# A first load of 8 rows for 16, and ScalarE's padding drains one row group sooner, in a low-rank-adapted linear layer

## The chip, the cores, the metric

One core of a Trainium2 chip. The metric is the device time of one execution in microseconds (us), the median of several runs. The profiled execution's span is some 1.3 us shorter than its time. All times inside a span count from the span's start.

## The reference

```python
# x: 16 x 2048 x 256 float32; W: 256 x 256; lora_A: 256 x 16; lora_B: 16 x 256; lora_E: 16; scale = 1.0
x_flat = x.reshape(-1, in_dim)
y = x_flat @ W
lora_out = ((x_flat @ lora_A) * lora_E) @ lora_B
y = y + scale * lora_out
```

The kernel folds the low-rank part into one 256 x 256 weight, `weff`, and then multiplies x by it. It reads 33.6 MB of x and writes 33.6 MB of y.

## The kernel before

32,768 rows are cut into 4 chunks, each of 64 rows on each of 128 partitions (8.4 MB). Three "homes" in on-chip memory hold a chunk each; y overwrites x in its home. A chunk is computed in 16 groups of 4 rows: GpSimd casts a group to bf16, TensorE transposes it, VectorE copies the result out of PSUM (the memory that TensorE writes), TensorE multiplies, ScalarE copies y back to the home. SyncE issues nearly all loads and stores, in the order of a list, on one queue, called the ring below; 16 transfer engines serve it.

```python
ORDER = [
    ("A",),
    ("L", 0, 0, 16), ("L", 0, 16, 40), ("L", 0, 40, 64),   # load chunk 0: rows 0 to 16, ...
    ("L", 1, 0, 32), ("L", 1, 32, 64),
    ("L", 2, 0, 64),
    ("S", 0, 0, 40), ("S", 0, 40, 64),                     # store chunk 0
    ("L", 3, 0, 32), ("L", 3, 32, 64),                     # into chunk 0's home
    ("S", 1, 0, 64), ("S", 2, 2, 62), ("S", 3, 0, 64),
]
HELD = (2, 0)                    # GpSimd holds chunk 2 back ...
HOLDERS = (("S", 0, 0, 40),)     # ... until this store has landed
VECTOR_DRAINS, GPSIMD_DRAINS, SCALAR_DRAINS = 12, 10, 22
# ... (cut)
    def drain(engine, n):
        for op, landed in loaded.items():
            if op[1:3] == HELD:
                engine.wait_ge(landed, 16)
        for _ in range(n):
            engine.drain()

    def scalar_program():
        # ... (cut: set-up loads of W, B, E)
        for g in range(N_GROUPS):
            c, b = g // GPC, g % GPC * CG
            if (c, b) == HELD:
                drain(scalar, SCALAR_DRAINS)
            scalar.wait_ge(s_y, g + 1)
            scalar.copy(out=home(c)[:, b:b + CG, :], in_=psum_y[g % NY][:]).then_inc(s_free[(g + NY) % UNROLL], 1)
            # ... (cut)
            if g in ends:
                scalar.drain().then_inc(s_done, 1)      # lets SyncE issue a store

    # TensorE, for each group i (cut): turn(i + 1, i), then multiply(i).
    # turn(i + 1) waits for GpSimd's cast of group i + 1; its last transpose waits for the y buffer of group i.
```

The wait of GpSimd at HELD is called the hold. The drains do no work. They pad each engine's stream of instructions, so that the place where one page of instructions ends and the next begins (a crossing) falls into the hold.

The edge rows of chunk 2 (0, 1, 62, 63) go out on GpSimd's own queue in three unequal shares.

## Time and profile before

| | before |
|---|---|
| time, median of 6 runs | 161.25 us (161.09 to 161.41) |
| span of the profiled run | 160.0 us |
| transfers, all queues, share of 16 engines' span | 98.9% |
| first landing of x / chunk 2 landed / first store landed | 8.09 / 62.70 / 75.04 us |
| ScalarE's drains | 80.23 to 81.42 us |
| last store issued / landed | 122.82 / 159.99 us |

Some numbers below come from the trace's packet records (start, duration, size and queue of each). "Excess" below is the time by which packets of 1024 bytes or more take longer than 9 ns + 0.03676 ns a byte (the line through the medians of 611 ns for 16,384 bytes and 2418 ns for 65,536), summed and divided by 16 engines.

### The profile page before, as it was taken

How to read it: one execution, taken by the hardware profiler on the slowest of the kernel's cores; microseconds unless marked ns; L12 is line 12 of the kernel's file. 1: busy time of each engine (PE TensorE's matmuls, PEld its weight loads, DVE VectorE, ACT ScalarE, POOL GpSimd, SP SyncE). 2: the span in 40 equal slices, each digit the busy share in tenths (PEclk: the TensorE clock that was granted, in tenths of full speed). 3: DMA queues.
4: the chain of work that ended last, by engine and by line, in shares of the span. 5: the costliest groups of instructions: out<-in, count | busy, mean ns of one | idle time of the engine just before them, and what ended most of it. 6: DMA issues, size and time to landing. Idle time of an engine off the chain costs nothing.

```text
span 160.0 us, 2070 instructions
## 1 busy us (share of the span) xinstructions
PE 96.5 (60%) x782; PEld 84.4 (53%) x782; DVE 45.4 (28%) x66; ACT 66.0 (41%) x65; POOL 69.3 (43%) x73
## 2 busy tenths in 40 slices
PE   2769999999999900000999999999994000000000
PEld 1246899999999900000789999999993000000000
DVE  0113355555555500000155555555550000000000
ACT  3001477777777720000257777777775000000000
POOL 1072577777787400002577777778762000000000
PEclk9999999999999995555599999999999555555555
DMA  7999999999969997999999999989979997989986
GB/s 269 427 448 436 412 440 467 451 393 418 631 262 524 475 311 328 403 420 434 412 465 428 401 475 426 532 377 410 524 308 446 480 485 305 544 342 481 441 360 262
DMA packets 2451, 67.43 MB, mean 421 GB/s; under 512 B 512, under 2 KB 528, under 8 KB 784
## 3 DMA queue, kind: packets, MB, share of 16 engines
q1 hardware_dynamic: 2016, 66.60, 97.4%
q0 software_dynamic: 224, 0.52, 0.9%
q10 hardware_dynamic: 208, 0.28, 0.6%
q14 instruction: 3, 0.02, 0.0%
HBM read 33.85 MB, written 33.55 MB: 421 GB/s over the span
## 4 chain that ended last, share of the span: by engine, by line
PE 38%; DMA 33%; ACT 3%; POOL 1%; issue 1%; ACTq 0%; SPq 0%
DMA out_dram<-home 28%; PE psum_y L269 24%; PE psum_xt L258 13%; DMA home<-in_x_dram 5%; ACT home L221 3%; POOL stage L200 1%; PE psum_y L291 1%; SPq L147 0%; ACTq L175 0%; ACTq L225 0%
## 5 line engine op out<-in xcount | busy, mean ns | idle before, releaser
L200 POOL CAST stage<-home 128x1024 bf16<-128x1024 f32 x64 | 66.6, 1042 | 48.6 <-PE psum_xt L258 22.1
L221 ACT COPY home<-psum_y 128x1024 f32<-128x1024 f32 x64 | 64.7, 1012 | 54.8 <-PE psum_y L269 54.8
L269 PE MATMUL psum_y<-weff,xt 128*128 128x256 bf16 x512 | 69.1, 280 | 0.0
L242 DVE COPY xt<-psum_xt 128x1024 bf16<-128x1024 bf16 x64 | 44.3, 692 | 66.2 <-PE psum_xt L258 66.2
L258 PE MATMUL psum_xt<-ident,stage 128*128 128x128 f32 x260 | 42.2, 286 | 22.3 <-POOL stage L200 22.3
L269 PEld LDWEIGHTS psum_y<-weff,xt 128*128 128x128 bf16 x512 | 51.5, 101 | 6.2
L258 PEld LDWEIGHTS psum_xt<-ident,stage 128*128 128x128 f32 x260 | 32.4, 148 | 25.2 <-issue 23.6
L282 PE MATMUL psum_y<-ident 128*128 128x512 f32 x4 | 3.8, 1101 | 2.9 <-POOL ident L180 2.9
L282 PEld LDWEIGHTS psum_y<-ident 128*128 128x128 f32 x4 | 1.2, 325 | 3.9 <-POOL ident L180 2.9
L230 DVE TENSOR_SCALAR ate<-psum_y,e_sb 16x256 f32<-16x256 f32 x1 | 0.5, 471 | 7.2 <-DMA e_sb<-in_lora_E_dram 7.2
L168 POOL DMA_DIRECT2D out_dram<-home x3 | 2.0, 676 | 1.0 <-PE psum_xt L258 1.0
L221 ACT ACT_TABLE_LOAD x1 | 1.3, 1283 | 2.1 <-SPq L304 2.1
L291 PE MATMUL psum_y<-b_sb,ate 16*128 16x256 f32 x4 | 2.1, 670 | 0.0
L291 PEld LDWEIGHTS psum_y<-b_sb,ate 16*128 16x128 f32 x4 | 1.2, 320 | 0.5 <-issue 0.3
L246 DVE TENSOR_TENSOR weff<-w_sb,psum_y 128x512 bf16<-128x512 f32 x1 | 0.7, 689 | 1.4 <-PE psum_y L291 1.4
L285 PEld LDWEIGHTS psum_y<-ident,a_sb 128*16 128x16 f32 x2 | 0.3, 138 | 1.2 <-issue 1.2
L178 POOL MEMSET ident<- 128x128 f32 x1 | 0.2, 205 | 1.7 <-SPq L304 1.7
L285 PE MATMUL psum_y<-ident,a_sb 128*16 128x128 f32 x2 | 0.6, 421 | 0.0
L180 POOL TENSOR_SCALAR_AFFINE_SELECT ident<-ident 128x128 f32<-128x128 f32 x1 | 0.3, 284 | 0.2 <-POOL ident L178 0.2
L326 POOL MEMSET const-float32-0.0<- 128x1 f32 x1 | 0.1, 94 | 0.2 <-issue 0.2
L326 POOL MEMSET const-bfloat16-1.0<- 128x1 bf16 x1 | 0.1, 97 | 0.0
L326 POOL MEMSET const-uint8-127<- 128x1 uint8 x1 | 0.1, 97 | 0.0
(1 smaller groups left out, 0.1 us busy)
## 6 DMA issues: line engine op xcount, KB each, us to landing
home<-in_x_dram SPq DMA_DIRECT2D x4, 4096.0 KB, 24.4
out_dram<-home SPq DMA_DIRECT2D x1, 7680.0 KB, 38.0
home<-in_x_dram SPq DMA_DIRECT2D x2, 3072.0 KB, 16.8
out_dram<-home SPq DMA_DIRECT2D x1, 5120.0 KB, 45.2
out_dram<-home SPq DMA_DIRECT2D x1, 3072.0 KB, 44.6
home<-in_x_dram SPq DMA_DIRECT2D x1, 2048.0 KB, 7.7
out_dram<-home POOLq DMA_DIRECT2D x1, 432.0 KB, 30.2
w_sb<-in_W_dram ACTq DMA_DIRECT2D x1, 256.0 KB, 2.8
```

Source lines behind the costliest of these rows:

```text
L168: engine.dma_start(out=ends_of(y_chunks[SHARED]), in_=ends_of(home(SHARED))).then_inc(landed, 16)
L200: gpsimd.tensor_copy(out=stage[g % NS][:], in_=home(c)[:, b:b + CG, :]).then_inc(s_stage[g % UNROLL], 1)
L221: scalar.copy(out=home(c)[:, b:b + CG, :], in_=psum_y[g % NY][:]).then_inc(s_free[(g + NY) % UNROLL], 1)
L230: vector.tensor_scalar(out=ate[:], in0=psum_y[0][:R, :KT, :P], scalar1=e_sb[:], scalar2=float(scale), op0=ALU.mult, op1=ALU.mult,).then_in ...
L242: vector.tensor_copy(out=xt[g % NX][:], in_=psum_xt[g % NT][:].bitcast(BF16)).then_inc(s_xt[g % UNROLL], 1)
L246: vector.tensor_add(out=weff[:], in0=w_sb[:], in1=psum_y[1][:, :KT, :]).then_inc(s_free[0], 1)
L258: ins = tensor.transpose(psum_xt[i % NT][:, b, :], words[:, b, :], ident[:])
L269: ins = tensor.matmul(psum_y[i % NY][:, b, :], xt[i % NX][:, b, t::KT], weff[:, t, :], start=(t == 0), stop=(t == KT - 1),)
L282: tensor.matmul(psum_y[1][:, :2, :], ident[:], ident[:, None, :].to_broadcast([P, 4, P]), start=True, stop=True)
L285: ins = tensor.transpose(psum_y[0][:R, t, :P], a_sb[:, t, :], ident[:])
L291: ins = tensor.matmul(psum_y[1][:, t, :], ate[:, t, :], b_sb[:], start=True, stop=True)
L326: nc = _bacc.Bacc("TRN2", target_bir_lowering=False, num_devices=1)
```

## The change

It is meant to start compute sooner, by a smaller first load, and to take ScalarE's drains off the path that leads out of the hold: they stand before the copy of group 31, which waits for the hold, instead of behind it.

```diff
-    ("L", 0, 0, 16),
-    ("L", 0, 16, 40),
-    ("L", 0, 40, 64),
+    ("L", 0, 0, 8),
+    ("L", 0, 8, 32),
+    ("L", 0, 32, 64),
@@
-SCALAR_DRAINS = 22
+SCALAR_DRAINS = 26
@@
-            if (c, b) == HELD:
+            if (c, b + CG) in (HELD, (HELD[0] - 1, HELD[1] + ROWS)):
                 drain(scalar, SCALAR_DRAINS)
```

## The prediction

> **What bounds the kernel now.** I first read the page's slices and its queue lines: is any engine, or the transfer engines, full for the whole span?
>
> ```profile
> PE   2769999999999900000999999999994000000000
> POOL 1072577777787400002577777778762000000000
> DMA  7999999999969997999999999989979997989986
> ...
> q1 hardware_dynamic: 2016, 66.60, 97.4%
> q0 software_dynamic: 224, 0.52, 0.9%
> q10 hardware_dynamic: 208, 0.28, 0.6%
> q14 instruction: 3, 0.02, 0.0%
> ```
>
> The compute engines have two empty stretches: a hold at about 57 to 75 us, and everything after 123 us. The DMA row has none, and its queues sum to 98.9% of 16 engines' span. The transfers are the bound: x in and y out, 67.1 MB that no part of this change alters. Is the rate full in every stage? Windows give, at the end of each line, granted clock, DMA share and GB/s (a packet counts where it begins, hence shares just over 1):
>
> ```profile
> 0.00:2.00 2.00, 0.00 (x0) 0.00 (x0) 0.00 (x0) 0.00 (x0) 0.20 (x4) 1.00 0.43 111
> 2.00:40.00 38.00, 34.86 (x239) 28.07 (x240) 14.60 (x22) 19.21 (x19) 22.57 (x24) 1.00 1.01 432
> 40.00:80.00 40.00, 19.99 (x167) 18.05 (x166) 9.43 (x15) 14.33 (x15) 14.28 (x15) 0.74 1.00 420
> 80.00:120.00 40.00, 39.95 (x366) 36.95 (x365) 21.15 (x31) 30.25 (x31) 31.18 (x31) 1.00 1.01 435
> 120.00:158.00 38.00, 1.71 (x16) 1.33 (x14) 0.26 (x1) 2.17 (x3) 1.07 (x2) 0.56 1.02 437
> ```
>
> The rate is the same with all engines computing (80 to 120) as with none (after 123). Counting packets in flight in the trace, an engine is idle only 1.33 us at the start and 0.81 us in the last 2 us. The weak row, 420 GB/s, holds one oddity: of the 65,536-byte packets, 2418 ns in the median, the 16 that begin at 58.0 to 58.5 us (the last of chunk 2's load, one on each engine) take 3339 to 3927 ns. That is 1.24 us in which all engines stand, and nothing in the trace names its cause.
>
> Then the chain of waits around the end of the hold, where ScalarE's drains stand now:
>
> ```profile
> 29.86 45.17 DMA out_dram<-home
> 75.04 0.05 issue
> 75.09 1.05 POOL stage L200
> ...
> 77.37 1.72 PE psum_y L269 x8
> 79.09 0.02 issue
> 79.11 1.01 ACT home L221
> ...
> 80.92 0.35 issue
> 81.27 0.14 ACTq L175
> 81.42 0.04 issue
> 81.45 1.02 ACT home L221
> ```
>
> TensorE turns group 32 before it multiplies group 31, and group 32 waits for the hold, so ScalarE's copy of group 31 comes only at 79.11. The 22 drains, ordered after that copy, run at 80.23 to 81.42 with compute waiting. The chain makes this look decisive, and it is where I distrust it: it passes through the issue of the last store at 122.82 us, which lands at about 160.0, 37 us later. Its own packets need 8 x 2418 ns = 19.3 us per engine. The other 17.9 us is queueing behind the stores of chunks 1 and 2. Compute has that much slack.
>
> **What the skill says.** The Trainium skill, "DMA: Bandwidth & Descriptors", section "Queues, rings and completion order": on each engine, descriptors are consumed in ring order. The trace agrees: the store that was issued at 29.86 sends its first packet at 61.59, when chunk 2's load is through. Section "Where 436 GB/s comes from" puts the fabric at 435 and HBM traffic at about 358. This trace has 432 to 437 in four of five stages, so here the fabric figure holds. "Runtime: NRT & Kernel Launch", section "Instruction fetch mechanics": each engine streams instructions in blocks, fetched by its own DMA while it runs, so the crossing is mostly hidden. The trace shows it: ScalarE's drains follow each other every 33 ns except one gap of 0.36 us before the last, and an 8192-byte packet of 309 ns on the instruction queue at 84.82. VectorE and GpSimd drain in the hold, from 62.72, and have theirs at 67.83 and 67.84. I read the drains as padding that puts each crossing into the hold; only ScalarE's misses it.
>
> **The change, part by part.**
>
> Loads of 8, 24 and 32 rows. Pieces, rows and bytes are unchanged, and each piece still puts 8 packets on each engine. Medians of the trace: 611 ns for 16 rows, 912 for 24, 1213 for 32, and 309 for 8192 bytes (the instruction packets), which is 8 rows. Before: 8 x (611 + 912 + 912) = 19.48 us. After: 8 x (309 + 912 + 1213) = 19.47 us. Gain 0.01 us.
>
> First landing: 8.09 - 8 x 0.302 = 5.7 us. Second: 15.40 - 2.4 = 13.0. Third: 22.70, unchanged. The first cast moves from 8.15 to about 5.7, but group 2 is now in the second piece. Its cast goes from 10.48 to 13.0, which still lets its transpose start at 14.1 instead of 15.24. Group 8 is in the third piece; its cast, at 22.71 now, can't come sooner. It ends 0.9 us ahead of its transpose at 24.66. So of a first lead of 2.4 us some 0.6 to 0.9 stays, the first store is issued at about 29.1 and TensorE reaches the hold as much earlier. Chunk 2's load still lands at 62.7 and the first store at 75.0, and both set the hold. Worth at the end: 0.
>
> Can the smaller first piece empty the ring? The second load is issued at 2.09; the first took 1.45 us from issue (0.43) to packet (1.88), so the second's packets are there at 3.55. The small first load keeps engines busy until 1.88 + 2.47 + about 0.8 for the set-up loads = 5.1. No.
>
> Drains. From before the copy of group 32 to before that of group 31, and 26 for 22. In the order of the trace, copy and drain of group 31 now follow them, so the crossing (the gap before entry 64 of ScalarE) falls before the 24th of 26. All run when chunk 2 lands, 62.7 to 64.1, with ScalarE waiting till 79.11 anyway. Removed from 80.23 to 81.42: 1.2 us of ScalarE. TensorE gains less: its multiply of group 32 ends at 80.83, so the copy starts then and not at 81.45, and TensorE's own wait for that copy is 0.29 us. Then 1.31 us per group as before: last copy 121.75 to about 121.4, last store issued at 122.5 for 122.82. That eats into nothing but the queueing of 17.9 us. Worth at the end: 0. The fetch of 309 ns moves from 84.8 to about 67.8 and stays one packet on one engine: 0.
>
> Sum: 161.23 - 0.01 - 0 - 0 = 161.2. I shade it to 161.1 for the odd stall: it may be tied to when compute stops, which moves.
>
> **Rivals.**
>
> 1. The chain is taken at its word: 0.6 to 0.9 us from the start and 0.3 to 1.2 from the drains, giving 159.1 to 160.3. For it: PE has 37% of the chain by its two main lines. Against: the ring is never empty from 1.9 to 159 us.
> 2. The stall of 1.24 us follows the timing of compute. It sits 1 to 4 us after compute stops, near the fall of the granted clock at 59.4. With the stop shifted it may go, giving 160.0. Against: the clock falls likewise at 124.2 with no such packets. I give this one in six.
> 3. The opening is hurt: smaller pieces interleave worse with W, A, B and E. The first eight-odd packets of 16,384 bytes already took 767 to 907 ns for 611. Excess in the first 5 us is 0.34 us per engine; were it doubled, 161.6.
> 4. The end loses balance. The chunk 2 edge rows go out from GpSimd's queue in three unequal shares, interleaved with the ring; issued 0.3 us sooner, they may meet other packets. The engines' last packets end at up to 159.66 against 0.81 us of mean idleness after 158; a shift of one share is under 0.3 us. Time 161.0 to 161.5.
>
> **Range and chances.** Three runs of before lie within 161.09 to 161.41. Rival 2 sets the low end, rivals 3 and 4 the high: 160.3 to 161.6. Two per cent is 3.2 us; all rivals together do not reach that. Faster 0.01, same 0.98, slower 0.01.
>
> **What would show it.** Right: DMA row and queue shares as now, first-piece packets of about 310 ns, landings at 5.7, 13.0 and 22.7, drains of ScalarE at 62.7 to 64.1, no gap of 1.2 us between its copies of groups 31 and 32, last store issued up to a microsecond sooner, and its landing, counted from issue, longer by just that. Wrong: an idle stretch of DMA near 4 us, a late first store, packets at 58 us back at 2418 ns, or an end that moves with the last issue.

## The result

161.33 us, the median of 6 runs (161.15 to 162.16), for 161.25: ratio 1.0013, 95% interval 0.999 to 1.0035. The time is the same. Ratios here and below are the mean time of one kernel's fast runs over that of the other's of the same rounds, so not quite the ratio of the medians quoted. A slow run (a lower granted clock, and over 1.5% above the fastest of its kernel) is left out; there was one, in the last experiment.

The page of the changed kernel, slices and queues:

```profile
PE   2974999999999900000999999999994000000000
POOL 1507468777787200002577777778762000000000
DMA  6999999999979997989999999997997997989976
...
q1 hardware_dynamic: 2016, 66.60, 97.3%
q14 instruction: 3, 0.02, 0.0%
```

Compute begins one slice sooner (POOL 5 for 0 and PE 9 for 7 in the second) and GpSimd then runs short of rows (the 0 in its third slice). The DMA row shows no gain anywhere. Its windows, the last columns again being clock, DMA share and GB/s:

```profile
2.00:40.00 38.00, 33.94 (x245) 27.65 (x246) 14.99 (x22) 19.56 (x20) 22.95 (x24) 0.96 1.01 432
40.00:80.00 40.00, 19.34 (x162) 17.41 (x160) 9.03 (x14) 13.98 (x14) 13.61 (x15) 0.75 1.01 425
80.00:120.00 40.00, 40.00 (x367) 37.15 (x366) 21.19 (x31) 30.39 (x31) 31.18 (x31) 1.00 1.03 446
120.00:158.00 38.00, 1.67 (x16) 1.30 (x13) 0.21 (x1) 2.12 (x3) 1.02 (x2) 0.56 0.98 422
```

Over 80 to 158 us the rate is the same as before: 446 and 422 for 435 and 437, where a packet of 65,536 bytes falls on one or the other side of a border. The weak second row is less weak, 425 for 420: the odd stand of all engines at 58 us has an excess of 0.86 us in this profile for 1.23. That is enough for the 0.2 us by which this profiled span (159.8) is shorter; it is the fastest of the six runs, and their median shows none of it. The clock column is to be read with care: where the trace has no clock record it reads 1.00. Before has none ahead of 18.42 us, and there eight matmuls take 1.71 us, against 0.87 at the full clock later.

What the loads did, in GpSimd's timeline (start, duration, and at the end of the line what it waited for). Before:

```profile
8.15 2.02 POOL L200 CAST stage<-home 128x1024 bf16<-128x1024 f32 x2 [5.32 <-DMA home<-in_x_dram]
...
22.71 1.04 POOL L200 CAST stage<-home 128x1024 bf16<-128x1024 f32 x1 [0.27 <-PE psum_xt L258]
```

After:

```profile
5.83 2.02 POOL L200 CAST stage<-home 128x1024 bf16<-128x1024 f32 x2 [3.01 <-DMA home<-in_x_dram]
13.12 3.01 POOL L200 CAST stage<-home 128x1024 bf16<-128x1024 f32 x3 [5.28 <-DMA home<-in_x_dram]
...
22.81 3.01 POOL L200 CAST stage<-home 128x1024 bf16<-128x1024 f32 x3 [1.17 <-DMA home<-in_x_dram]
```

The first cast comes 2.3 us sooner, but the second and third piece are waited for now, 5.28 and 1.17 us. Group 8's cast starts at 22.8 in both kernels. 0.64 us of lead is left when the first store is issued, at 29.22 for 29.86. That these 0.64 us come from the loads is not shown: in the eight other profiles below that keep the first loads of before and whose edits act only later, this store is issued at 27.01 to 29.73. It goes with the moment at which the full clock comes to stay: 13.98 us for 27.01, 18.42 in before. At a like moment (18.26 to 18.89) two profiles with 16 rows have 29.73 and 29.86, two with 8 rows 29.59 and 29.22; so a few tenths of lead may be the loads'.

What the drains did, in the chain of waits (the work that ended last, followed back to what each step waited for) after the change:

```profile
29.22 45.82 DMA out_dram<-home
75.04 0.05 issue
75.09 1.05 POOL stage L200
...
79.08 0.85 PE psum_xt L258 x4
79.93 1.13 PE psum_y L269 x8
81.06 0.44 PE psum_xt L258 x4
```

The first store is issued sooner and lands at 75.04 as before: the 0.64 us went into its wait in the ring. (To the hundredth that is chance. With the loads of before a store issued at 27.01 landed at 75.59.) The drains are gone from the chain. They ran at 62.25 to 63.57 (chunk 2 landed at 62.23), with the crossing before the 24th. Yet the last store is issued at 122.78 for 122.82. TensorE's timeline shows where the gain out of the hold went. Before:

```profile
79.72 1.11 PE L269 MATMUL psum_y<-weff,xt 128*128 128x256 bf16 x8
80.67 0.60 PE L258 MATMUL psum_xt<-ident,stage 128*128 128x128 f32 x4
```

After:

```profile
79.72 1.34 PE L269 MATMUL psum_y<-weff,xt 128*128 128x256 bf16 x8
80.90 0.60 PE L258 MATMUL psum_xt<-ident,stage 128*128 128x128 f32 x4
```

The same eight matmuls, begun at the same 79.72, took 0.23 us longer, because the full clock came back at 80.32 us in this execution for 79.86 in the other.

### The profile page after: what moved, and what is told of

It is laid out like the page before. It is cut to its first block, busy times and chain, and to the rows that moved or that the text cites. A ratio compares the mean times of both kernels' runs of the same rounds, so it can differ in the third digit from the quotient of the medians.

```text
span 159.8 us, 2074 instructions
## 1 busy us (share of the span) xinstructions
PE 94.9 (59%) x782; PEld 83.5 (52%) x782; DVE 45.4 (28%) x66; ACT 66.1 (41%) x65; POOL 69.0 (43%) x73
## 4 chain that ended last, share of the span: by engine, by line
PE 37%; DMA 36%; POOL 1%; ACT 1%; issue 0%; SPq 0%; ACTq 0%
DMA out_dram<-home 29%; PE psum_y L269 24%; PE psum_xt L258 13%; DMA home<-in_x_dram 7%; POOL stage L200 1%; ACT home L221 1%; ACTq L225 0%; SPq L340 0%; SPq L304 0%
## 5 line engine op out<-in xcount | busy, mean ns | idle before, releaser
L258 PE MATMUL psum_xt<-ident,stage 128*128 128x128 f32 x260 | 41.5, 284 | 23.8 <-POOL stage L200 23.5
L291 PE MATMUL psum_y<-b_sb,ate 16*128 16x256 f32 x4 | 1.4, 478 | 0.0
```

Source lines behind the costliest of these rows:

```text
L258: ins = tensor.transpose(psum_xt[i % NT][:, b, :], words[:, b, :], ident[:])
L291: ins = tensor.matmul(psum_y[1][:, t, :], ate[:, t, :], b_sb[:], start=True, stop=True)
```

## The experiments

My theory: the ring of transfers on SyncE's queue sets the end, and compute has slack of many microseconds behind it, so that neither half of the change can reach the end. Its main rival: the chain of waits at its word, with compute on the path. Twelve kernels ran, all correct, in four calls; the kernels of one call share a chip and its runs of the kernel before. The intervals are 95%. Edits are against the kernel before; some are put on fewer lines.

### The loads alone

```diff
-    ("L", 0, 0, 16), ("L", 0, 16, 40), ("L", 0, 40, 64),
+    ("L", 0, 0, 8), ("L", 0, 8, 32), ("L", 0, 32, 64),
```

> The loads of 8, 24 and 32 rows alone, drains as before. Theory (the ring of transfers sets the end, compute has slack): ratio 1.000, within 0.3%; first landing near 5.8 us, first store issued near 29.2, hold released at 75.0, drains back at about 80.2 to 81.4 and TensorE waiting for the copy behind them. Rival (the chain at its word): the first store 0.6 us sooner is 0.6 us at the end, ratio 0.996.

Measured: 161.31 us for 161.26, ratio 1.0024 (0.9995 to 1.0052). First landing 5.73 (5.78 in the full change), first store issued at 29.59, hold released at 75.19. No gain; and two of six runs, 161.83 and 162.64, are above all eleven of before. That is taken up in the last experiment.

### The drains alone

```diff
-SCALAR_DRAINS = 22
+SCALAR_DRAINS = 26
-            if (c, b) == HELD:
+            if (c, b + CG) in (HELD, (HELD[0] - 1, HELD[1] + ROWS)):
```

> The earlier drains alone, loads as before. Theory: ratio 1.000, within 0.3%; no drains between the copies of groups 31 and 32; last store issued 0 to 0.4 us sooner than 122.82, how much depending on when the granted clock of TensorE comes back (79.9 before, 80.3 after). Rival (the chain at its word): 1.2 us of drains go from the path, ratio 0.993.

Measured: 161.27 us for 161.26, ratio 1.0000 (0.9987 to 1.0013). The expectation of a last store 0 to 0.4 us sooner missed: it was issued at 124.00, 1.2 us later. Here the hold was released at 75.60 and the full clock came back only at 82.24. So the clock's return moves compute by more than the drains do, and the end follows neither.

### Chunk 0 in one load

The opposite of the change: compute can start only when all 64 rows are there.

```diff
-    ("L", 0, 0, 16), ("L", 0, 16, 40), ("L", 0, 40, 64),
+    ("L", 0, 0, 64),
```

> Chunk 0 in one load of 64 rows, the opposite of the change: the first cast can start only at about 22.7 us, 14.5 us later than before, and compute runs some 9 to 13 us later until the hold. Theory: the hold is still released at about 75 us by the first store (issued near 42, first packet still near 61.6 when the loads are through), so the end does not move: 161.0 to 161.6. Rival (an early start is worth its time at the end): 169 to 175 us.

Measured: 161.37 us for 161.26, ratio 1.0007 (0.9993 to 1.0022). GpSimd's and SyncE's timelines of this run:

```profile
22.76 2.02 POOL L198 CAST stage<-home 128x1024 bf16<-128x1024 f32 x2 [19.93 <-DMA home<-in_x_dram]
```

```profile
43.46 8.20 SPq L159 DMA_DIRECT2D out_dram<-home  x2
74.60 8.00 SPq L154 DMA_DIRECT2D home<-in_x_dram  x2
```

The first cast comes 14.6 us later than before, the first store is issued 13.6 us later, and still it lands by 74.60. A start 14.6 us later costs nothing, so one 2.3 us sooner can gain nothing by way of compute.

### A dose of delay behind the hold: 386 and 786 drains

```diff
-SCALAR_DRAINS = 22
+SCALAR_DRAINS = 386
```

> 364 more drains at the old place, 12.1 us at 33.3 ns each on the path of compute behind the hold. Theory: compute's slack is the 139.5 us at which the ring finishes chunk 2's store, less 1.5 us from issue to first packet, less the issue at 122.8, so 15.2 us; 12.1 us fit: last store issued at about 134.9, end unmoved, 161.0 to 161.7. Rival (the drains are on the path that sets the end): 173 us.

Measured: 162.77 us for 161.26, ratio 1.0090 (1.0075 to 1.0105). Neither theory: 1.5 us of a delay of 15.7 arrived at the end, where the slack was to swallow all. Three parts of my sum were off. The drains took longer than 33.3 ns each, for the stream stops at two further crossings (0.54 and 1.16 us), and ScalarE's next copy started 14.05 us later than before, not 12.1. While they ran, TensorE stood and its granted clock fell to half, from 86.32 to 99.98 us; the groups behind the drains cost 1.6 us more by that. So the last store was issued at 138.51 and not 134.9. And the page had six instruction packets for three:

```profile
q14 instruction: 6, 0.05, 0.1%
```

The packet records name no engine, but strung together, each packet to the one that ends where it starts, they give 16 sequences. In that of this run that ends last, at 161.06, sit four packets of instructions; the mean sequence ends at 159.56.

```diff
-SCALAR_DRAINS = 22
+SCALAR_DRAINS = 786
```

> 764 more drains at the old place, 25.4 us, more than the slack of 15.2 us. Theory: the ring runs dry twice, at about 119.7 us (the store of chunk 2 issued near 127.3) and again before the last store, issued near 148.2; from there 1.5 us to the first packet, 19.3 us of packets, 0.4 us to the end and 1.2 us outside the span: 170 to 171 us, and DMA slices with holes near 120 to 128 and 147 to 150. Rival (the drains are on the path one for one): 186.7 us.

Measured: 179.26 us for 161.08, ratio 1.1138 (1.1121 to 1.1154). The DMA slices have the hole:

```profile
DMA  7999989989969999899999999960005999689995
```

The ring ran dry, at about 120 us as expected, and once more before the last store. The size missed, by the delay: with five crossings more of 0.4 to 2.4 us each the drains made ScalarE's next copy 32.1 us late, the half clock (87.77 to 118.49 us) made it 34.0, and the last store was issued at 156.78, not 25.4 us late. From that issue the span ends 20.8 us later, near the 21.2 expected. So of 34.0 us of lateness the span shows 17.5, and the slack is 16.4 us.

### The two causes in the 386-drain run, one at a time

Delay without instructions:

```diff
                 drain(scalar, SCALAR_DRAINS)     # (the new semaphore's line is cut)
+                for i in range(20):
+                    if i:
+                        scalar.wait_ge(s_spare, i)
+                    scalar.copy(out=w_sb[:], in_=w_sb[:]).then_inc(s_spare, 1)
```

(A first build without the waits was refused, by my account, for a race between one copy's read and the write of the one before. It did not run and is not on record.)

> The same delay of compute behind the hold as in the run with 386 drains (its last store was issued at 138.5), but by 20 copies of 128x512 on ScalarE with a wait after each, some 12 to 15 us, and so without further pages of instructions. Theory A (that run's 1.5 us come from its three further instruction packets, 0.93 us, on one transfer engine, which ends last at 161.05 where the mean engine ends at 159.56): with as late a last store and no further packets the time is 161.1 to 161.6. Theory B (they come from the last store being issued too late for the ring): 162.4 to 162.9 if it is issued at 138 or later.

Measured: 161.92 us for 161.04, ratio 1.0050 (1.0036 to 1.0065), with the last store issued at 138.39 and three instruction packets. An excess of 0.75 us stands at 137.5 to 140 us, where the last store's packets should follow chunk 2's; before has none there, the 386-drain run 0.44. An issue at 138.4 is at the edge of the slack.

Instructions without delay:

```diff
-SCALAR_DRAINS = 22
+SCALAR_DRAINS = 390
-            if (c, b) == HELD:
+            if (c, b + CG) in (HELD, (HELD[0] - 1, HELD[1] + ROWS)):
```

> 390 drains at the changed kernel's place, in the hold: they run from 62.7 to about 78, before ScalarE's next copy at 79.1, so compute is not delayed and the last store is issued at 122.5 to 123. Theory A (further instruction packets on one engine): three more packets of 309 ns, that engine ends about 1 us behind the others, time 162.0 to 162.6, ratio 1.005 to 1.009. Theory B (lateness of the last store): ratio 1.000.

Measured: 162.07 us for 161.04, ratio 1.0056 (1.0042 to 1.0071). The last store is issued at 122.74, no later than before, and the instruction queue has three packets more:

```profile
q14 instruction: 6, 0.05, 0.1%
```

The last sequence ends at 160.61, again the one with four packets of instructions, and the mean at 159.02. So both theories hold a part: 0.5% for lateness, 0.6% for three packets of instructions; the 386-drain run has both, at 0.9%. The second part is the one that nobody waits for in any view of waits: it only makes one transfer engine later than its fifteen fellows.

### GpSimd no longer holds chunk 2 for the store

```diff
-HOLDERS = (("S", 0, 0, 40),)
+HOLDERS = ()
```

> GpSimd no longer waits for the first store before group 32, only for chunk 2's load: compute behind the hold starts at 62.7 instead of 75.1 and the last store is issued near 110 instead of 122.8. Theory: the ring is full anyway, so nothing is gained, ratio 0.997 to 1.003 (a loss would mean that compute beside the stores costs them time, which the windows do not show). Rival (compute is on the path): 12 us faster, ratio 0.93.

Measured: 161.32 us for 161.08, ratio 1.0015 (1.0002 to 1.0028). Compute behind the hold started when chunk 2 had landed (62.57) and GpSimd had drained, at 63.33 for 75.09; the last store was issued at 118.3, 4.5 us sooner and not near 110, for chunk 3's second load lands only at about 102. A start twelve microseconds earlier behind the hold gained nothing. Compute is off the path in this direction too.

### The first store ahead of chunk 2's load

```diff
-    ("L", 2, 0, 64),
     ("S", 0, 0, 40),
+    ("L", 2, 0, 64),
```

> The first store stands in the ring ahead of chunk 2's load. Same bytes, the hold still released near 75 (by chunk 2's load). It asks for the cause of the 0.9 to 1.2 us in which all 16 engines stand near 58 to 61 us. If it belongs to the first turn from loads to stores, the long packets are the last of chunk 1's load, at 40 to 42 us, and the time is the same. If it belongs to the moment at which compute stops (57 us), it stays at 58 to 61, now within chunk 2's load. If it needs both, it is gone, and the time is 0.9 to 1.2 us shorter, ratio 0.993.

Measured: 162.29 us for 161.08, ratio 1.0082 (1.0064 to 1.0100). The long packets are gone from 58 us and stand at 37.5 to 42.5, all in chunk 1's last load, the last before the store: an excess of 1.04 us up to 40 and 0.32 after. So the stand of all engines goes with the first turn from loads to stores, not with the moment when compute stops. The one-load kernel agrees: TensorE was computing through 58 us there, and the excess was 0.85. The mechanism is not settled: the later turn from loads to stores, at about 101 us, has no such excess. Why this order costs 0.8% I did not settle either; its profile has more turns and its last packet at 160.35, 1 us after the mean engine's.

### A first write at the start of the run

```diff
+        ins = scalar.dma_start(out=y_chunks[N_CHUNKS - 1, :, 0, :8], in_=W[:P, :8]).then_inc(s_first, 16)
+        opening.append(ins.ins.name)          # ahead of the loads of W, B, E
@@ before the last store (the new semaphore's line is cut)
+                    sync.wait_ge(s_first, 16)
```

> A transfer of 32 bytes a row, 128 rows, from W into a corner of the output (stored again with the right values at the end), issued first of all on ScalarE's queue, so that the run's first write to memory comes at 1 to 2 us and not at 58 to 61. The run with the store moved ahead showed that the stand of all engines goes with the first turn from loads to stores. Theory A (it is paid by the first write): the long packets at 58 us go, and if the early write finds the engines idle the time falls by up to 1.1 us, ratio 0.993; if it stops the loads as long, the stand only moves to the first 5 us, ratio 1.000. Theory B (it belongs to the turn of a full ring): the packets at 58 us stay near 3500 ns, ratio 1.000 to 1.002.

Measured: 161.39 us for 161.04, ratio 1.0018 (1.0003 to 1.0032). The excess at 58 us fell to 0.47 (it is 0.84 to 1.23 in the twelve other profiles that have this turn there and not elsewhere), and that of the first 10 us rose to 0.67 (0.16 to 0.56 in the others): several first packets of x took 1136 to 1401 ns, where before had at most 907. It looks as if part of the stand moved to the opening, and none was saved. That speaks for theory A without the gain, but 0.47 us are left, so a first write is not the whole cause. And the edit also delayed the set-up loads and SyncE's second issue (2.98 for 2.09 us), so the longer first packets are not shown to be the stand. The first multiplication by weff began at 20.24 us for 13.54, and that again did not show at the end.

### No padding at all

```diff
-VECTOR_DRAINS = 12 / GPSIMD_DRAINS = 10 / SCALAR_DRAINS = 22
+VECTOR_DRAINS = 0 / GPSIMD_DRAINS = 0 / SCALAR_DRAINS = 0
```

> No padding drains on ScalarE, VectorE or GpSimd. Theory: the end does not move, 161.0 to 161.6: their page crossings fall into the computing after the hold and cost each engine some 0.4 us once, inside the slack of 15 us; the instruction packets of 8192 bytes appear later than 67.8 us, three still. Rival (the padding keeps a fetch from standing behind the ring for long): an engine stands for several us at its crossing, and even then the end moves only if that is over 15 us.

Measured: 160.93 us for 161.08, ratio 0.9990 (0.9975 to 1.0004). The three instruction packets came at 79.5, 88.6 and 105.5 us, and the last store was issued at 122.11. The padding as a whole buys nothing here, so moving a part of it had nothing to gain. This is the lowest time, but not clear of the kernel before; no version tried beats both kernels.

### A first piece of 4 rows

```diff
-    ("L", 0, 0, 16), ("L", 0, 16, 40), ("L", 0, 40, 64),
+    ("L", 0, 0, 4), ("L", 0, 4, 32), ("L", 0, 32, 64),
```

> Loads of 4, 28 and 32 rows, drains as before: half the first piece of the change again. In the 12 runs with a first piece of 8 rows there were three between 161.8 and 162.7 us, in 29 of before none over 161.41. Theory (the ring never runs empty: 8 x 159 ns of rows and 0.8 us of set-up loads from about 2.1 us reach past 3.7, where the second load's packets begin): ratio 0.999 to 1.002, the high runs are chance or another cause. Rival (a small first piece hurts the opening): an idle stretch of the engines at 3 to 4 us in the profile, ratio 1.003 or more, and several runs over 161.8.

Measured: 162.34 us (161.75 to 163.03) for 161.21 (160.82 to 161.46, and a slow run of 163.64 that is left out), ratio 1.0077 (1.0053 to 1.0102). The rival is right in the size and wrong in the way: the opening is hurt, but no idle stretch stands at 3 to 4 us. What the packets show is spread. When the 16 sequences reach the third piece they lie 0.86 us apart for 0.46 before; at the first store 1.41 for 0.74; at the end 1.28 for 0.96, with the mean end the same, 159.2, and the last one at 160.05 for 159.66. That is 0.4 us of the 1.1: the profiled execution was also the fastest of the six, so the rest is not seen. Nor is the spread shown to be the cause: the one-load kernel ends 1.20 apart at a ratio of 1.0007. The runs with 8 rows fit between (0.50 and 0.75 us apart at the third piece, ratios 1.0013 and 1.0024). Three of their twelve are above 161.8, and none of the 39 fast runs of before is above 161.46 (the 163.64 has a granted clock of 0.695 for 0.80 to 0.83); but their intervals include 1.

## Why the prediction was right, point by point

**The bound.** Right, and now tested in both directions: a start 14.6 us later, and one 12 us earlier behind the hold, and neither moved the end. A slip in the reading: the windows show 432 to 437 GB/s in three of five rows, not four; the others are 111, in the first 2 us, and 420.

**The size of the loads.** Right. The 8-row packets have a median of 309 ns, and the pieces landed at 5.78, 13.07 and 22.75 us for 5.7, 13.0 and 22.7 predicted. The first store was issued at 29.22 for 29.1, but there the agreement is in part luck: with the loads of before it came at 27.0 to 29.9, as the clock had it, and the sum has no term for that. That the ring makes up for any such lead was right: issued between 27.01 and 43.46, in this order of the ring, it landed at 74.6 to 76.1.

**The drains.** The move was right: in the hold, crossing before the 24th of 26. The term "TensorE's own wait for that copy is 0.29 us", which was to bring the last issue to 122.5, did not come through: 122.78. What it left out is the clock. The Trainium skill, "TensorE: Matmul & The Clock Gate", section "What's actually happening", says that the clock is granted by a free-running window of 3413 ns. The traces agree: the granted clock changes after 3.41, 6.83, 20.48 or 40.96 us, all multiples of it, and came back at 79.86, 80.32 and 82.24 us in three executions whose hold ended at 75.04, 75.04 and 75.60. Its phase outweighs 0.29 us. The end did not care.

**The slack.** Mis-sized. "Compute has that much slack" was 17.9 us, the last store's 37.2 us less its own packets. The run with 786 drains gives 16.4, and an issue 15.6 us later than before already costs something. The sum forgot the time from issue to first packet (0.83 us in that run) and from the last packet to the span's end (0.39), and that a ring refilled at the last moment loses some time (0.75 us of excess in the run with 20 copies).

**Rival 1, the chain at its word.** Refuted by the loads alone, the drains alone, the one load and the run without the hold: none moved the end as the chain has it.

**Rival 2, the stand at 58 us tied to when compute stops.** Refuted: it follows the first turn from loads to stores, for a reason that stays open. The 0.1 us by which I shaded the estimate on its account had no ground; 161.2 would have been nearer to 161.33.

**Rival 3, the opening hurt by smaller pieces.** I held it for a matter of interleaving and put it at 161.6 at most. At 4 rows it is real, 0.8%; at 8 rows 0.1 to 0.2% that the intervals don't separate from nothing. So the half of the change that was to gain at the start more likely costs a little.

**Rival 4, the balance at the end.** Not seen for the change itself, which keeps three instruction packets. But its mechanism, one engine late and the rest waiting, is what three more of them showed: 0.6%.

## What to carry to other kernels

When the transfer queues sum to 99% of the span, a chain of waits that runs through compute into an issue says only who issued last. Take the last store's time from issue to landing, subtract its own packets, and you have about the slack that any saving in compute will vanish in (17.9 us so, 16.4 by test); delay compute on purpose to check it. What did move this end is what one of the 16 transfer engines has to carry: three instruction packets more on one engine cost 0.6%, where a start of compute 12 us earlier gained nothing. A first piece of 4 rows cost 0.8%, in a way that is only partly seen.

## What the Trainium skill lacked or had wrong

- "DMA: Bandwidth & Descriptors", section "Where 436 GB/s comes from": it lets HBM bind at about 358 GB/s for such transfers; the four windows of 38 to 40 us shown for each kernel have 420 to 446 GB/s. The 425 GB/s that the same section quotes as measured fits them.
- No page that I read has a cost for the first turn of a full ring from loads to stores: 0.84 to 1.23 us of all 16 engines near 58 us, and 1.4 us at 37.5 to 42.5 when a store is moved ahead.
- "Runtime: NRT & Kernel Launch", section "Instruction fetch mechanics": it has blocks of 256 instructions (16 KiB) and crossings that are mostly hidden. Here the stops in ScalarE's stream come every 128 entries of the trace, with one packet of 8192 bytes each, and last 0.36 to 2.35 us in a run of drains; whether the smaller block is a setting, no run shows. What it lacks: in the 386-drain run four such packets sat in one transfer engine's sequence, the one that ended last, and three further ones cost 0.6% with nobody waiting for them.
